# Seven-product block steps for a third of the feed-forward products of a 256-token encoder block

## The chip, the cores and the metric

The kernel runs on one core of one Trainium2 chip. The metric is device time in microseconds (us) of one launch; the time of a kernel is the median of its runs. Beside it there is one profiled execution with its own length, the span.

## The reference

One layer on 256 tokens of width 2048, in float32. Two feed-forward half-steps stand around a mixer:

```python
def rmsnorm(x, g):
    y = x * lax.rsqrt(jnp.mean(x * x, axis=-1, keepdims=True) + EPS)
    return y * g

def swiglu(h, w1, w3, w2):
    return (jax.nn.silu(h @ w1) * (h @ w3)) @ w2

x = x + 0.5 * swiglu(rmsnorm(x, ffn1_norm_g), ffn1_w1, ffn1_w3, ffn1_w2)
h = rmsnorm(x, mix_norm_g)
# projections h @ w_in, differential attention y_a, latent attention y_b
merged = sigmoid(ga) * (y_a @ w_branch_a) + sigmoid(gb) * (y_b @ w_branch_b)
x = x + merged @ w_out
x = x + 0.5 * swiglu(rmsnorm(x, ffn2_norm_g), ffn2_w1, ffn2_w3, ffn2_w2)
```

`w1` and `w3` are 2048 x 5632, `w2` is 5632 x 2048. The change touches the two `swiglu` half-steps; the mixer between them computes what it did.

## The kernel before, in words

**Products.** TensorE (PE) multiplies in float32r, a shortened float32, so every large product runs as three passes. An operand v is split into hi (v cast to float32r) and lo = v - hi, and hi*hi, hi*lo and lo*hi accumulate in one PSUM bank. The activations are the stationary operand: 128 x 128 blocks, transposed, already split. The weights are the moving operand, 128 rows by 512 columns in a matmul.

**One tile of weights.** `gemm` (line 124) walks down the rows of a weight matrix, two blocks of 128 rows at a time. SyncE (SP) issues a DMA of 512 KB into a raw tile, of which there are four (L135). `split` casts it on ScalarE (ACT, L105) and subtracts on VectorE (DVE, L106) into the tiles `wh` and `wl`, of which there are three each. Then come 12 matmuls: two row blocks, two blocks of 128 tokens, three passes (L144, L145, L146). Behind each tile one pending step of other work is issued, in the order in which steps were put off (`later`).

**A half-step.** `ffn` (line 231) cuts the 5632 hidden columns into 11 chunks of 512. A chunk is a gemm with `w1` (8 tiles, names f_u), Silu on ACT (L242), a gemm with `w3` (8 tiles, names f_v), and the product of the two on DVE (L246). Its transposes and their split (names f_t, f_ga, f_gb, f_gc) are put off into the next gemms. When all 44 blocks of hidden activations G are there, four gemms with `w2` over 22 tiles each follow (names f_d), and L261 adds half of the result to x, which stays in SBUF throughout. So a half-step has 11 x 16 + 4 x 22 = 264 tiles.

**What sets the order.** Each engine has its own queue and runs it in order. The order within a queue is that of the code as the scheduler lays it out; where an instruction needs another engine's result it waits on a semaphore, and everything behind it on its engine waits with it. Two PSUM banks of a gemm are in use while two others are free for the next, so that a gemm can begin before the last one has been read.

Of the kernel before, what the change touches and what calls it, by code (L numbers as in the profile page):

```python
# [71 lines left out]
def tile_block(ctx: ExitStack, tc: tile.TileContext, a, out: bass.AP):  # L72
# [51 lines left out]
    def gemm(w, n, kbs, hi, lo, name, due=None):  # L124
        """[S, n] = act @ w: w holds the rows of the blocks kbs, one block of 128 after
        another; hi/lo(kb, t) give the stationary operands.  Behind each weight tile
        one pending step of other work is issued; before tile `due` all of them."""
        po = [psum("mm", 4, f"{name}_{t}") for t in range(NT)]
        wv = w.rearrange("(kb p) n -> p kb n", p=P)
        for k0 in range(0, len(kbs), KT):  # L130
            if due is not None and k0 // KT == due:
                flush()
            kt = min(KT, len(kbs) - k0)
            raw = wp.tile([P, KT, n], F32, tag="raw", bufs=4, name=f"{name}_w")
            nc.sync.dma_start(out=raw[:, :kt], in_=wv[:, k0:k0 + kt, :])  # L135
            wh = wp.tile([P, KT, n], F32R, tag="wh", name=f"{name}_h")
            wl = wp.tile([P, KT, n], F32R, tag="wl", name=f"{name}_l")
            split(wh[:, :kt], wl[:, :kt], raw[:, :kt])
            for j in range(kt):
                kb = kbs[k0 + j]  # L140
                first, last = k0 + j == 0, k0 + j == len(kbs) - 1
                for t in range(NT):
# [2 lines left out]
                    nc.tensor.matmul(out=o, lhsT=hi(kb, t), rhs=wl[:, j], start=False, stop=False)  # L145
                    nc.tensor.matmul(out=o, lhsT=lo(kb, t), rhs=wh[:, j], start=False, stop=last)  # L146
# [79 lines left out]
    def chunk_done(x, t, c, T, g, pool, name):
        chunk_put(x, t, c, T, g, pool, name)
        chunk_sum(x, t, c, pool, name)

    # ---------------------------------------------------------------- feed forward  # L230
    def ffn(x, T, rstd, w1, w3, w2, tags, pool, done, name, first=None):
        hi, lo = operand(T)
        nf = DFF // P
        G = [big_tile(tags[0], f"{name}_ga"), big_tile(tags[1], f"{name}_gb"),
             pool.tile([P, 2, nf - 2 * KD, S], F32R, name=f"{name}_gc")]
        for c in range(DFF // NW):
            cs = slice(c * NW, (c + 1) * NW)
            p1 = first if c == 0 and first else gemm(w1[:, cs], NW, allk, hi, lo, f"{name}_u{c}")
            sg = []
            for t in range(NT):  # L240
                s = pool.tile([P, NW], F32, tag="silu", bufs=3, name=f"{name}_s{c}{t}")
                nc.scalar.activation(out=s, in_=p1[t], func=AF.Silu, scale=rstd[:, t:t + 1])  # L242
                sg.append(s)
            p3 = gemm(w3[:, cs], NW, allk, hi, lo, f"{name}_v{c}")
            for t in range(NT):
                nc.vector.scalar_tensor_tensor(out=sg[t], in0=p3[t], scalar=rstd[:, t:t + 1], in1=sg[t],  # L246
                                               op0=ALU.mult, op1=ALU.mult)

            def put(c, t, s):
                tp = transposes(lambda i: s[:, i * P:(i + 1) * P], 4, f"{name}_t{c}{t}")  # L250
                g, kk, sl = G[4 * c // KD], 4 * c % KD, slice(t * P, (t + 1) * P)
                split(g[:, 0, kk:kk + 4, sl], g[:, 1, kk:kk + 4, sl], tp)

            later(wait, *(partial(put, c, t, sg[t]) for t in range(NT)))
        ghi = lambda kb, t: G[kb // KD][:, 0, kb % KD, t * P:(t + 1) * P]
        glo = lambda kb, t: G[kb // KD][:, 1, kb % KD, t * P:(t + 1) * P]
        for c in range(D // NW):
            cs = slice(c * NW, (c + 1) * NW)
            po = gemm(w2[:, cs], NW, list(range(nf)), ghi, glo, f"{name}_d{c}", due=8)
            for t in range(NT):  # L260
                nc.vector.scalar_tensor_tensor(out=x[:, t, cs], in0=po[t], scalar=0.5, in1=x[:, t, cs],  # L261
                                               op0=ALU.mult, op1=ALU.add)
                done(t, c)
# [4 lines left out]
    with tc.tile_pool(name="f1", bufs=1) as pool:
        x = pool.tile([P, NT, D], F32, name="x1")
        T = big_tile("A", "hT1")  # L270
        def fetch(c):
            for t in range(NT):
                cs = slice(c * NW, (c + 1) * NW)
                nc.sync.dma_start(out=x[:, t, cs], in_=xin[:, t, cs])

        def put(c):
            for t in range(NT):
                chunk_put(x, t, c, T, "ffn1_norm_g", pool, f"i{c}{t}")

        rstd, step = rms_of_x("n1")  # L280

        def sums():
            for c in range(D // NW):
                for t in range(NT):
                    chunk_sum(x, t, c, pool, f"i{c}{t}")
            step()

        def start():
            for c in range(1, D // NW):
                fetch(c)  # L290
            put(1)

        fetch(0)
        gain_columns(0)
        put(0)
        later(start, wait, partial(put, 2), wait, partial(put, 3), sums, partial(gain_columns, 1))
        Tm = []

        def done1(t, c):
            if not Tm:  # L300
                Tm.append(big_tile("A", "hTm"))
            cs = slice(c * NW, (c + 1) * NW)
            nc.sync.dma_start(out=xdram[:, t, cs], in_=x[:, t, cs])
            later(partial(chunk_done, x, t, c, Tm[0], "mix_norm_g", pool, f"m{c}{t}"))

        ffn(x, T, rstd, a["ffn1_w1"][0], a["ffn1_w3"][0], a["ffn1_w2"][0], ("C", "D"), pool, done1, "f1")
        rstd, step = rms_of_x("n2")
        later(step)
        w_in = a["w_in"][0]
        hi, lo = operand(Tm[0])  # L310
        c_job = lambda j: gemm(w_in[:, O_C + j * 448:O_C + (j + 1) * 448], 448, allk, hi, lo, f"c{j}", due=4)
        first = c_job(0)

# [364 lines left out]
```

## Time and profile before

| | |
|---|---|
| median of 3 runs | 2444.77 us (2444.17 to 2445.04) |
| the profiled execution (its span) | 2442.6 us |
| feed-forward tiles, both half-steps | 528 |
| DMA, mean over the span | 185 GB/s |

The span begins with the program and ends with the last output transfer. A busy share counts an engine as busy while an instruction runs on it. PE records overlap, since matmuls are pipelined, so the pace of PE is read from the distance between the starts of instructions that follow it and not from the length of one record. In a table of waits a row names the waiting engine and what it waited for; then come the total, the number of times and the longest wait. SPq and POOLq are the queues of transfers that SyncE and GpSimd issue.

### The profile page before, as it was taken

What the parts mean: (1) busy time and instruction counts of PE and PEld (TensorE: products, weight loads), DVE (VectorE), ACT (ScalarE), POOL (GpSimd) and SP (SyncE); (2) the same over time, 40 slices, a digit from 0 to 9 for tenths busy, and PEclk for the clock granted to TensorE, in tenths of its full rate; (3) what the DMA queues carried; (4) which work ended last, traced back from release to release, by engine and by line L of the source; (5) the groups of instructions that cost most, each with busy time, mean ns of one, the idle gap of its engine ahead of it and who ended that gap; (6) DMA issues with size and microseconds to landing.
All of it is one profiled execution on the core that took longest, in us unless ns stands there. A gap on an engine that the chain in (4) does not pass through costs nothing.

```text
span 2442.6 us, 29136 instructions
## 1 busy us (share of the span) xinstructions
PE 2429.4 (99%) x11070; PEld 2013.9 (82%) x11070; DVE 1324.6 (54%) x1865; ACT 1111.9 (46%) x1378; POOL 96.0 (4%) x144
## 2 busy tenths in 40 slices
PE   8999999999999999999999999999999999999999
PEld 7888888888889888888888888888888888888887
DVE  5445445445555666666665665655545545444444
ACT  5444444434444555545545554444444444443333
POOL 1000000000000100001111210000000000000000
PEclk9999999999999999999999999999999999999999
DMA  7666666666667655655554556666666666666664
GB/s 222 186 190 191 188 190 189 190 190 199 199 200 202 186 164 171 179 168 164 150 158 151 156 157 183 189 223 184 188 190 190 189 190 189 188 191 190 202 205 153
DMA packets 235867, 450.92 MB, mean 185 GB/s; under 512 B 14612, under 2 KB 27600, under 8 KB 235600
## 3 DMA queue, kind: packets, MB, share of 16 engines
q1 hardware_dynamic: 234432, 448.40, 61.4%
q8 instruction: 86, 1.41, 0.2%
q10 hardware_dynamic: 1008, 0.66, 0.1%
q14 instruction: 53, 0.43, 0.1%
q0 software_dynamic: 288, 0.03, 0.0%
HBM read 444.83 MB, written 4.19 MB: 184 GB/s over the span
## 4 chain that ended last, share of the span: by engine, by line
PE 41%; issue 9%; POOL 2%; DVE 1%; DMA 0%; ACT 0%; POOLq 0%; ACTq 0%; DVEq 0%
PE f_u L146 3%; PE f_u L144 3%; PE f_u L145 3%; PE f_v L144 3%; PE f_v L145 3%; PE f_v L146 3%; PE f_d L146 3%; PE f_d L144 3%; PE f_d L145 3%; PE wo L146 1%; PE wo L144 1%; PE wo L145 1%; PE bb L146 1%; PE bb L144 1%; PE bb L145 1%
## 5 line engine op out<-in xcount | busy, mean ns | idle before, releaser
L106 DVE TENSOR_TENSOR f_v_l<-f_v_w,f_v_h 128x1024 fp32r<-128x1024 f32 x176 | 215.5, 1225 | 261.3 <-ACT f_v_h L105 261.3
L106 DVE TENSOR_TENSOR f_d_l<-f_d_w,f_d_h 128x1024 fp32r<-128x1024 f32 x176 | 215.7, 1225 | 243.3 <-ACT f_d_h L105 243.3
L106 DVE TENSOR_TENSOR f_u_l<-f_u_w,f_u_h 128x1024 fp32r<-128x1024 f32 x176 | 215.6, 1225 | 220.8 <-ACT f_u_h L105 220.8
L105 ACT CAST f_d_h<-f_d_w 128x1024 fp32r<-128x1024 f32 x176 | 185.6, 1055 | 289.2 <-PE f_d L146 276.0
L105 ACT CAST f_u_h<-f_u_w 128x1024 fp32r<-128x1024 f32 x176 | 185.3, 1053 | 282.5 <-PE f_u L146 175.6
L105 ACT CAST f_v_h<-f_v_w 128x1024 fp32r<-128x1024 f32 x176 | 185.1, 1053 | 239.6 <-PE f_v L146 168.3
L144 PE MATMUL f_u<-f_u_h,hT 128*128 128x512 f32 x704 | 278.4, 396 | 0.0
L145 PE MATMUL f_u<-f_u_l,hT 128*128 128x512 f32 x704 | 274.7, 390 | 0.5 <-DVE f_u_l L106 0.5
L146 PE MATMUL f_u<-f_u_h,hT 128*128 128x512 f32 x704 | 274.9, 391 | 0.0
L144 PE MATMUL f_v<-f_v_h,hT 128*128 128x512 f32 x704 | 273.9, 389 | 0.0
L145 PE MATMUL f_v<-f_v_l,hT 128*128 128x512 f32 x704 | 273.9, 389 | 0.0
L146 PE MATMUL f_v<-f_v_h,hT 128*128 128x512 f32 x704 | 273.9, 389 | 0.0
L146 PEld LDWEIGHTS f_u<-f_u_h,hT 128*128 128x128 f32 x704 | 132.3, 188 | 28.0
L145 PEld LDWEIGHTS f_u<-f_u_l,hT 128*128 128x128 f32 x704 | 132.6, 188 | 27.2 <-DVE f_u_l L106 0.7
L146 PEld LDWEIGHTS f_v<-f_v_h,hT 128*128 128x128 f32 x704 | 132.2, 188 | 27.5
L144 PEld LDWEIGHTS f_v<-f_v_h,hT 128*128 128x128 f32 x704 | 132.2, 188 | 27.4
L145 PEld LDWEIGHTS f_v<-f_v_l,hT 128*128 128x128 f32 x704 | 132.2, 188 | 27.4
L144 PEld LDWEIGHTS f_u<-f_u_h,hT 128*128 128x128 f32 x704 | 132.3, 188 | 26.1
L144 PE MATMUL da<-da_h,hTm 128*128 128x512 f32 x256 | 103.9, 406 | 0.0
L144 PE MATMUL f_d<-f_d_h,f_ga 128*128 128x512 f32 x256 | 100.5, 393 | 0.0
L146 PE MATMUL da<-da_h,hTm 128*128 128x512 f32 x256 | 100.2, 391 | 0.0
L106 DVE TENSOR_TENSOR da_l<-da_w,da_h 128x1024 fp32r<-128x1024 f32 x64 | 78.2, 1223 | 40.5 <-ACT da_h L105 40.1
(313 smaller groups left out, 4765.2 us busy)
## 6 DMA issues: line engine op xcount, KB each, us to landing
f_u_w<-in_ffn_w SPq DMA_DIRECT2D x176, 512.0 KB, 3.8
f_v_w<-in_ffn_w SPq DMA_DIRECT2D x176, 512.0 KB, 3.7
f_d_w<-in_ffn_w SPq DMA_DIRECT2D x176, 512.0 KB, 4.3
da_w<-in_w_in SPq DMA_DIRECT2D x64, 512.0 KB, 3.8
dav_w<-in_w_in SPq DMA_DIRECT2D x32, 512.0 KB, 3.8
ga_w<-in_w_in SPq DMA_DIRECT2D x32, 512.0 KB, 3.7
ba_w<-in_w_branch_a SPq DMA_DIRECT2D x32, 512.0 KB, 4.1
gb_w<-in_w_in SPq DMA_DIRECT2D x32, 512.0 KB, 4.3
```

What stands on the lines that cost most here:

```text
L105: nc.scalar.copy(out=hi, in_=src)
L106: nc.vector.tensor_sub(out=lo, in0=src, in1=hi.bitcast(F32))
L144: nc.tensor.matmul(out=o, lhsT=hi(kb, t), rhs=wh[:, j], start=first, stop=False)
L145: nc.tensor.matmul(out=o, lhsT=hi(kb, t), rhs=wl[:, j], start=False, stop=False)
L146: nc.tensor.matmul(out=o, lhsT=lo(kb, t), rhs=wh[:, j], start=False, stop=last)
```

## The change

**Two by two blocks.** The feed-forward products go through a new function, `gemm2`. It computes two output column halves of 512 (left and right) for both token blocks in one go. In the up-projection left is `w1` and right is `w3`; in the down-projection they are neighbouring halves of 1024 columns of `w2`. It walks down the rows in pairs of blocks, so a pair is a 2 x 2 block product: two token blocks by two row blocks, and two row blocks by two column halves. A pair is of one of two kinds.

- Kind P has the 8 block products of the textbook, 24 matmuls.
- Kind S has 7 block products of sums of blocks (Strassen's method in Winograd's form), 21 matmuls. Its weight sums are formed on the way in and its activation sums beforehand. Seven PSUM banks q1 to q7 hold the sums of products, one bank each and no second set, and are combined when they are read. Kind P adds into the banks q2 to q5 and uses differences of activation blocks, so that both kinds share the same reading.

**Which pairs.** An up-projection of 512 hidden columns has 8 pairs in the order PSPPSPSP, so 3 of 8 are S. The down-projection no longer waits for all of d_ff: after up-chunks 2, 5, 8 and 10 the `w2` rows of the chunks done so far are multiplied (6, 6, 4 and 6 pairs, 2, 2, 1 and 2 of them S, since the kinds by chunk are PS, PP, SP), once for each 1024 output columns. A half-step is thus 11 + 8 = 19 calls with 132 pairs, 47 of them S; both half-steps have 38 calls, 264 pairs and 94 S.

**The weight sums of an S pair.** Seven blocks are loaded instead of four. SP loads two right blocks into `sm` (L315, 512 KB), the second right block once more (L316, 256 KB) and two left blocks (L319, 512 KB). Two DMAs that GpSimd (POOL) issues add a block each to the two in `sm` (L321, L322: `accum_op=ALU.add`, 256 KB each). DVE makes the other two sums (L325, L326). Then four blocks of `raw` and three of `sm` are split. There are three raw, `wh` and `wl` tiles of four blocks each (twice as large as before); an S pair takes one raw and two of `wh` and `wl`. There are two `sm` tiles.

**Partial sums.** x no longer stays in SBUF. The result of a down-projection chunk other than the last is added to x in DRAM (`x_mid`) by an accumulating DMA from POOL, 1 MB each, 6 in a half-step (L421). For the last chunk x is loaded back in pieces (L393) and added on DVE.

**Small edits.** The factor 0.5 moves into the copy of the transposed hidden activations (L272, on ACT). Some tiles outside the half-steps go from two to one; the mixer's gemms keep their tiles of two blocks, now as halves of larger ones. The transposed sums of the second half-step's input are made while `w_out` is multiplied.

The diff, cut to its core (of the unchanged helpers and of the mixer nothing is shown):

```diff
+    SEVEN = (("q1", 0, "s", 1), ("q6", 5, "s", 0), ("q7", 2, "w", 1), ("q5", 4, "w", 0),
+             ("q2", 1, "s", 2), ("q3", 6, "s", 3), ("q4", 3, "w", 2))
+    PLAIN = (("q5", 2, 0), ("q2", 0, 1), ("q3", 4, 0), ("q4", 2, 1))
+    def put_pairs(pairs, srcs, gain, name):
...
+            tp = transposes(lambda i: src[:, i * P:(i + 1) * P], 4, f"tp_{name}{t}")
...
+                nc.scalar.activation(out=o, in_=i_, func=AF.Copy, scale=0.5)
...
+                if kind == "S":
+                    nc.vector.tensor_sub(out=g[:, 4], in0=g[:, 2], in1=g[:, 3])
+                    nc.vector.tensor_sub(out=g[:, 5], in0=g[:, 4], in1=g[:, 0])
+                    nc.vector.tensor_add(out=g[:, 6], in0=g[:, 1], in1=g[:, 5])
+                    nc.vector.tensor_sub(out=g[:, 2], in0=g[:, 0], in1=g[:, 2])
+                    n = 7
+                else:
+                    nc.vector.tensor_sub(out=g[:, 4:6], in0=g[:, 0:2], in1=g[:, 2:4])
+                    n = 6
+                split(T[:, 0], T[:, 1], g[:, :n])
+    def gemm2(left, right, pairs, name, due=None, x=None):
...
+            if kind == "S":
+                sm = pools["w7"].tile([P, 3, NW], F32, tag="sum", bufs=2, name=f"{name}_s")
+                nc.sync.dma_start(out=sm[:, 0:2], in_=right(k))
+                nc.sync.dma_start(out=raw[:, 3], in_=right(k)[:, 1])
+            else:
+                nc.sync.dma_start(out=raw[:, 0::3], in_=right(k))
+            nc.sync.dma_start(out=raw[:, 1:3], in_=left(k))
+            if kind == "S":
+                nc.gpsimd.dma_start(out=sm[:, 0], in_=left(k)[:, 0], accum_op=ALU.add)
+                nc.gpsimd.dma_start(out=sm[:, 1], in_=right(k)[:, 0], accum_op=ALU.add)
...
+                nc.vector.tensor_add(out=raw[:, 0], in0=sm[:, 0], in1=raw[:, 3])
+                nc.vector.tensor_add(out=sm[:, 2], in0=raw[:, 0], in1=raw[:, 2])
...
+                split(sh, sl, raw)
+                wh, wl = h4("w")
+                split(wh[:, 0:3], wl[:, 0:3], sm)
...
+            if i == lastS:
+                nc.scalar.copy(out=e11, in_=q["q1"])
+                nc.vector.tensor_add(out=e12, in0=q["q6"], in1=e11)
+                nc.vector.tensor_add(out=e21, in0=q["q7"], in1=e12)
...
+        nc.vector.tensor_sub(out=e12, in0=q["q5"], in1=e12)
+            nc.vector.tensor_sub(out=e22, in0=q["q5"], in1=e21)
...
+        nc.vector.tensor_add(out=x11, in0=q["q2"], in1=x11)
+        nc.vector.tensor_add(out=x12, in0=q["q3"], in1=x12)
+        nc.vector.tensor_add(out=x21, in0=q["q4"], in1=x21)
+    TKINDS, GKINDS = "PSPPSPSP", ("PS", "PP", "SP")
+    DOWN = {2: (0, 1, 2), 5: (3, 4, 5), 8: (6, 7), 10: (8, 9, 10)}
...
+                    nc.gpsimd.dma_start(out=xdram[:, :, ns], in_=ev, accum_op=ALU.add)
```

**How the queues change.** First VectorE of the kernel before, from the w1 gemm of one chunk to that of the next, in the first half-step. f_u_l and f_v_l are the subtractions of the weight split, f_s the gated product of a chunk, f_gb the split of its transposes.

```order
L106 TENSOR_TENSOR f_ga<-f_t_1504,f_ga 128x4x128
L106 TENSOR_TENSOR f_u_l<-f_u_w,f_u_h 128x1024 x2
L106 TENSOR_TENSOR f_v_l<-f_v_w,f_v_h 128x1024 x8
L106 TENSOR_TENSOR f_u_l<-f_u_w,f_u_h 128x1024 x2
L246 SCALAR_TENSOR_TENSOR f_s_1601<-f_v_0_1605,rstd_n_90,f_s_1601 128x512
L246 SCALAR_TENSOR_TENSOR f_s_1603<-f_v_1_1606,rstd_n_90,f_s_1603 128x512
L106 TENSOR_TENSOR f_u_l<-f_u_w,f_u_h 128x1024 x3
```

The same engine of the changed kernel where the up-projection of chunk 3 (f1_u3) meets that of chunk 4 (f1_u4). Names with _w_ are raw tiles, _s_ the tiles of sums, lp the lo part of a P pair, ls that of an S pair's raw tile, q the banks, e the tile into which they are read.

```order
L325 TENSOR_TENSOR f1_u4_w_1926<-f1_u4_s_1927,f1_u4_w_1926 128x512
L121 TENSOR_TENSOR f1_u3_lp_1844<-f1_u3_w_1840,f1_u3_hp_1843 128x2048
L343 TENSOR_TENSOR f1_u3_e_1598<-f1_u3_q6_1596,f1_u3_e_1598 128x512
L326 TENSOR_TENSOR f1_u4_s_1927<-f1_u4_w_1926 128x512
L344 TENSOR_TENSOR f1_u3_e_1598<-f1_u3_q7_1597,f1_u3_e_1598 128x512
L121 TENSOR_TENSOR f1_u4_lp_1892<-f1_u4_w_1888,f1_u4_hp_1891 128x2048
L352 TENSOR_TENSOR f1_u3_e_1598<-f1_u3_q5_1595,f1_u3_e_1598 128x512
L354 TENSOR_TENSOR f1_u3_e_1598<-f1_u3_q5_1595,f1_u3_e_1598 128x512
L359 TENSOR_TENSOR f1_u3_e_1598<-f1_u3_q2_1592,f1_u3_e_1598 128x512
L360 TENSOR_TENSOR f1_u3_e_1598<-f1_u3_q3_1593,f1_u3_e_1598 128x512
L361 TENSOR_TENSOR f1_u3_e_1598<-f1_u3_q4_1594,f1_u3_e_1598 128x512
L121 TENSOR_TENSOR f1_u4_ls_1936<-f1_u4_w_1926,f1_u4_hs_1935 128x2048
```

Where there was a plain run of subtractions with two products in it, the queue now holds the first sum of chunk 4's first S pair (L325) ahead of the subtraction for the last P pair of chunk 3, and the seven readings of the banks of chunk 3 among the subtractions for chunk 4.

Next TensorE. In the kernel before, a stretch of a w1 gemm with four transposes in it; f_u_0 and f_u_1 are the banks of the two token blocks.

```order
L144 MATMUL f_u_1_506<-f_u_h,hT_89 128x512
L145 MATMUL f_u_1_506<-f_u_l,hT_89 128x512
L146 MATMUL f_u_1_506<-f_u_h,hT_89 128x512
L158 MATMUL f_t_568<-ident,f_s_355 128x128 x4
L144 MATMUL f_u_0_505<-f_u_h,hT_89 128x512
L145 MATMUL f_u_0_505<-f_u_l,hT_89 128x512
L146 MATMUL f_u_0_505<-f_u_h,hT_89 128x512
```

In the changed kernel the end of the first S pair of a chunk and the beginning of the P pair behind it. hs, ls and hw, lw are the parts of the two split tiles of an S pair, hp and lp those of a P pair.

```order
L305 MATMUL f_u_q_1882<-f_u_hs,hT1s 128x512
L305 MATMUL f_u_q_1882<-f_u_ls,hT1s 128x512
L305 MATMUL f_u_q_1882<-f_u_hs,hT1s 128x512
L305 MATMUL f_u_q_1883<-f_u_hw,hT1s 128x512
L305 MATMUL f_u_q_1883<-f_u_lw,hT1s 128x512
L305 MATMUL f_u_q_1883<-f_u_hw,hT1s 128x512
L173 MATMUL tp_f_1964<-ident,f_u_e 128x128 x4
L305 MATMUL f_u_q_1884<-f_u_hp,hT1p 128x512
L305 MATMUL f_u_q_1884<-f_u_lp,hT1p 128x512
L305 MATMUL f_u_q_1884<-f_u_hp,hT1p 128x512 x2
```

A split tile now feeds 24 matmuls (P), 12 (the raw tile of an S pair) or 9 (its sums), where each fed 12 before.

More of the change, by code (lines that the diff above doesn't have):

```diff
@@ L52 @@
 NW = 512
-KT = 2
+KT = 4
 MASKED = -1.0e30
@@ L129, in gemm @@
         wv = w.rearrange("(kb p) n -> p kb n", p=P)
-        for k0 in range(0, len(kbs), KT):
-            if due is not None and k0 // KT == due:
+        for k0 in range(0, len(kbs), 2):
+            if due is not None and k0 // 2 == due:
                 flush()
[L133 to L138, printed above, removed]
+            kt = min(2, len(kbs) - k0)
+            if k0 % KT == 0:
+                full = [wtile("raw", F32, f"{name}_w"), wtile("wh", F32R, f"{name}_h"), wtile("wl", F32R, f"{name}_l")]
+            raw, wh, wl = (f[:, k0 % KT:k0 % KT + kt, :n] for f in full)
+            nc.sync.dma_start(out=raw, in_=wv[:, k0:k0 + kt, :])
+            split(wh, wl, raw)
             for j in range(kt):
@@ L226, in chunk_done @@
[L226 to L236, printed above, removed]
-            cs = slice(c * NW, (c + 1) * NW)
-            p1 = first if c == 0 and first else gemm(w1[:, cs], NW, allk, hi, lo, f"{name}_u{c}")
-            sg = []
-            for t in range(NT):
[L241 to L263, printed above, removed]
@@ L265, in tile_block @@
-    xdram = nc.dram_tensor("x_mid", (P, NT, D), F32, kind="Internal").ap()
[L268 to L312, printed above, removed]
@@ new lines, in pair_views, with turn, sums @@
+    def pair_views(t, n, w):
+        return [t[:, i * 2 * w:(i + 1) * 2 * w, :].rearrange("p (h s) k -> p h s k", h=2) for i in range(n)]
+    def put_pairs(pairs, srcs, gain, name):
+        f = []
+        def turn(t):
+            if t == 0:
+                f.append(pools["pt"].tile([P, 2, 7, P], F32, tag="pf", bufs=1, name=f"pf_{name}"))
+            src = srcs(t)
+            tp = transposes(lambda i: src[:, i * P:(i + 1) * P], 4, f"tp_{name}{t}")
+            o, i_ = f[0][:, :, 2 * t:2 * t + 2], tp.rearrange("p (a b) k -> p a b k", a=2)
+            if gain is None:
+                nc.scalar.activation(out=o, in_=i_, func=AF.Copy, scale=0.5)
+            else:
+                nc.vector.tensor_tensor(out=o, in0=i_, in1=gain.rearrange("p (a b) -> p a b", a=2).unsqueeze(3)
+                                        .to_broadcast([P, 2, 2, P]), op=ALU.mult)
+        def sums():
+            for a, (kind, T, _) in enumerate(pairs):
+                g = f[0][:, a]
+                if kind == "S":
[8 more added lines that the diff above has]
+                split(T[:, 0], T[:, 1], g[:, :n])
+        return [partial(turn, t) for t in range(NT)] + [sums]
@@ new lines, in tile_block, with fetch @@
+    xdram = nc.dram_tensor("x_mid", (P, NT, D), F32, kind="Internal").ap()
+    f1 = ExitStack()
+    enter(f1, "w7", bufs=1)
+    enter(f1, "ev", bufs=1)
+    enter(f1, "acc", bufs=1, space=bass.MemoryType.PSUM)
+    pool = pools["pt"] = f1.enter_context(tc.tile_pool(name="f1", bufs=1))
+    x = big.tile([P, NT, D], F32, tag="D", name="x1")
+    T = ffn_T("C", "A", "hT1")
+    def fetch(c):
+        for t in range(NT):
+            cs = slice(c * NW, (c + 1) * NW)
+            nc.sync.dma_start(out=x[:, t, cs], in_=xin[:, t, cs])
@@ new lines, in put, with sums @@
+    def put(c):
+        return ffn_put(x, T, c, "ffn1_norm_g", f"i{c}")
+    rstd, step = rms_of_x("n1")
+    def sums():
+        for c in range(D // NW):
+            for t in range(NT):
+                chunk_sum(x, t, c, f"i{c}{t}")
+        step()
+        nc.gpsimd.dma_start(out=xdram, in_=x)
+    fetch(0)
+    gain_columns(0)
+    for s in put(0):
+        s()
+    run = lambda *ss: (lambda: [s() for s in ss])
+    later(run(partial(fetch, 1), *put(1)), run(partial(fetch, 2), partial(fetch, 3)), run(*put(2)), run(*put(3)), sums,
+          partial(gain_columns, 1))
@@ new lines, in tile_block, with done1 @@
+    Tm = []
+    def done1(x, t, c):
+        if not Tm:
+            Tm.append(big_tile("A", "hTm"))
+        cs = slice(c * NW, (c + 1) * NW)
+        nc.gpsimd.dma_start(out=xdram[:, t, cs], in_=x[:, t, cs])
+        later(partial(chunk_done, x, t, c, Tm[0], "mix_norm_g", f"m{c}{t}"))
+    ffn(T, rstd, a["ffn1_w1"][0], a["ffn1_w3"][0], a["ffn1_w2"][0], "D", "C", pool, done1, "f1")
+    f1.close()
+    del pools["acc"], pools["w7"]
+    mixps = ExitStack()
+    enter(mixps, "ps", bufs=2, space=bass.MemoryType.PSUM)
@@ L315, in tile_block @@
+    ptx = ExitStack()
+    enter(ptx, "pt", bufs=1)
+    rstd, step = rms_of_x("n2")
+    later(step)
+    w_in = a["w_in"][0]
+    hi, lo = operand(Tm[0])
+    c_job = lambda j: gemm(w_in[:, O_C + j * 448:O_C + (j + 1) * 448], 448, allk, hi, lo, f"c{j}", due=4)
+    first = c_job(0)
+    ptx.close()
     ctx_merge = ExitStack()
@@ L360, in rotate @@
             h = ROPE // 2
-            u = pool.tile([P, 2, 2, ROPE], F32, tag="rot", bufs=2, name=f"u_{name}")
+            u = pool.tile([P, 2, 2, ROPE], F32, tag="rot", bufs=1, name=f"u_{name}")
             for i in range(2):
```

153 lines of the change are left out of this document (130 added, 23 removed).

## The prediction

> **What bounds the kernel now.** I read the busy shares first.
>
> ```profile
> span 2442.6 us, 29136 instructions
> PE 2429.4 (99%) x11070; PEld 2013.9 (82%) x11070; DVE 1324.6 (54%) x1865; ACT 1111.9 (46%) x1378; POOL 96.0 (4%) x144
> ```
>
> PE is busy for 99% of the span; VectorE (DVE) and ScalarE (ACT) have half of it free. Overlapping records can hide gaps, so the second view is busy time by stretches: PE, PEld, DVE, ACT, POOL, the granted clock, the DMA share, GB/s.
>
> ```profile
> 0.00:20.00 20.00, 12.89 (x56) 9.92 (x57) 11.83 (x17) 8.90 (x11) 4.96 (x14) 1.00 0.78 249
> 0.00:40.00 40.00, 32.89 (x144) 26.16 (x145) 22.41 (x28) 24.36 (x40) 8.24 (x22) 1.00 0.76 238
> 40.00:500.00 460.00, 460.00 (x2068) 380.66 (x2067) 228.99 (x207) 197.19 (x207) 0.00 (x0) 1.00 0.64 189
> ```
>
> The clock is full. All idle time of PE lies in the first 20 us: 40 - 32.89 = 7.1 us; the next 460 us have none. The waits say who is early.
>
> ```profile
> ACT f_d_h L105 <- PE f_d L146: 276.0, 167, 1.7
> DVE f_v_l L106 <- ACT f_v_h L105: 261.3, 173, 3.7
> SPq L135 <- DVE f_u_l L106: 418.8, 176, 4.2
> PE f_u L145 <- DVE f_u_l L106: 0.5, 1, 0.5
> ```
>
> Everybody waits for PE: ACT for a free split tile, DVE for ACT, the loads for a free raw tile; PE waits for weights once in 176 f_u tiles, for 0.5 us. So PE's instruction count sets the time. Its pace is the distance between subtractions in the down-projection, one per 12 matmuls:
>
> ```profile
> 519.58 1.23 DVE L106 TENSOR_TENSOR f_d_l<-f_d_w,f_d_h 128x1024 fp32r<-128x1024 f32 x1 [1.50 <-ACT f_d_h L105]
> 522.30 1.23 DVE L106 TENSOR_TENSOR f_d_l<-f_d_w,f_d_h 128x1024 fp32r<-128x1024 f32 x1 [1.50 <-ACT f_d_h L105]
> ```
>
> 2.72 us for 12, or 0.2267 us a matmul.
>
> **What goes.** Three gemms of 176 tiles with 12 matmuls are 6336 matmuls. The 94 S pairs leave out 3 each: 282 x 0.2267 = **-63.9 us**. Nothing overlaps with this term, since PE is the path. A P pair takes 24 x 0.2267 = 5.44 us, an S pair 4.76.
>
> **What DVE and ACT get.** The rows for their pieces (mean ns behind the comma):
>
> ```profile
> L106 DVE TENSOR_TENSOR f_u_l<-f_u_w,f_u_h 128x1024 fp32r<-128x1024 f32 x176 | 215.6, 1225 | 220.8 <-ACT f_u_h L105 220.8
> L106 DVE TENSOR_TENSOR f_v_l<-f_v_w,f_v_h 128x1024 fp32r<-128x1024 f32 x176 | 215.5, 1225 | 261.3 <-ACT f_v_h L105 261.3
> L106 DVE TENSOR_TENSOR f_d_l<-f_d_w,f_d_h 128x1024 fp32r<-128x1024 f32 x176 | 215.7, 1225 | 243.3 <-ACT f_d_h L105 243.3
> L106 DVE TENSOR_TENSOR mq_l<-mq_w,mq_h 128x768 fp32r<-128x768 f32 x24 | 23.0, 958 | 27.1 <-ACT mq_h L105 27.1
> L534 DVE TENSOR_TENSOR mg<-ba,mg 128x512 f32<-128x512 f32 x8 | 5.5, 690 | 2.8 <-PE ba L146 2.8
> L106 DVE TENSOR_TENSOR ybT<-mo,ybT 128x256 fp32r<-128x256 f32 x16 | 6.7, 418 | 0.2 <-ACT ybT L105 0.2
> L109 DVE SCALAR_TENSOR_TENSOR jda<-qk 128x128 bf16<-128x128 f32 x64 | 18.5, 289 | 5.2 <-ACT qk L411 3.6
> L246 DVE SCALAR_TENSOR_TENSOR f_s<-f_v,rstd_n,f_s 128x512 f32<-128x512 f32 x44 | 30.9, 744 | 0.0
> L105 ACT CAST f_u_h<-f_u_w 128x1024 fp32r<-128x1024 f32 x176 | 185.3, 1053 | 282.5 <-PE f_u L146 175.6
> L105 ACT CAST mq_h<-mq_w 128x768 fp32r<-128x768 f32 x24 | 20.0, 835 | 25.1 <-issue 16.2 <-ACT me L585 3.6 <-PE dav L146 3.5
> L242 ACT ACTIVATE f_s<-f_u,rstd_n 128x512 f32<-128x512 f32 x44 | 29.9, 690 | 19.7 <-PE f_u L146 19.7
> ```
>
> From 768 to 1024 elements DVE needs 267 ns more, 1.043 ns an element: a subtraction of 2048 is 2.29 us, of 1536 1.76, an addition of 512 0.69. ACT's cast grows by 0.85 ns an element: 1.93 and 1.49 us. An S pair costs DVE 2 x 0.69 + 2.29 + 1.76 = 5.43 us, longer than its own 4.76 us on PE; a P pair 2.29. One up-projection call of 5 P and 3 S: 27.7 us of these, 7 bank readings (4.8), 2 products (1.5), and the hidden activations' sums (one of 256 elements at 0.42, four of 128 at 0.29) and two splits (about 1.05 each), 3.7: 37.7 us. PE takes 183 x 0.2267 + 8 transposes of about 0.11 = 42.4 us. DVE goes from half to 89%, ACT stays near 60%. On average both still hide. Not at each place: the lo part of a P pair behind an S pair comes after 5.43 us of DVE work while PE has 4.76, so it uses up what was ahead; and the banks have no second set, so a new call's first use of q5 waits for L354. Walking through one call by these durations I get 0.2 us of stall (a choice of order, so an estimate).
>
> **Loads.** The rows (median us to landing; then the queue's packets, MB and share of 16 engines):
>
> ```profile
> f_u_w<-in_ffn_w SPq DMA_DIRECT2D x176, 512.0 KB, 3.8
> f_d_w<-in_ffn_w SPq DMA_DIRECT2D x176, 512.0 KB, 4.3
> x<-in_x SPq DMA_DIRECT2D x8, 256.0 KB, 7.1
> x_mid<-x SPq DMA_DIRECT2D x8, 256.0 KB, 5.1
> grow<-in_mix_norm_g POOLq DMA_DIRECT2D x1, 8.0 KB, 2.8
> grow<-in_mla_k_norm_g POOLq DMA_DIRECT2D x1, 0.5 KB, 7.1
> q1 hardware_dynamic: 234432, 448.40, 61.4%
> 1.29 0.72 POOL L187 DMA_DIRECT2D grow<-in_mix_norm_g  x1 [0.46 <-issue]
> ```
>
> A packet is 2 KB and takes 0.614 x 16 x 2442.6 / 234432 = 0.102 us of one engine. A P pair is 512 packets, an S pair 896, so a call's 5248 packets take 33.6 of its 42.4 us on 16 engines, 79% (before, 64% in the second stretch). That fits, with later landings. [...]
>
> Two places are tight. L325 stands in DVE's queue ahead of the last P pair's subtraction, and waits for L316, whose raw tile comes free only three pairs earlier: by my walk it has about 3.1 us, and 256 KB should land in about 3 (an estimate below the 3.8 of 512 KB; under crowding 5.1 and 7.1 are seen). Each us too late stalls DVE, and soon PE, at up to two places in an up-projection call. The accumulating pair has a chain of its own: load of `sm` (3.8 to 4.3), two issues on GpSimd (up to 0.72 each), landing (unknown: 2.8 to 7.1 by the nearest rows, small ones): 8 to 13 us, against about 13 from when L315 can go out. I take 5 us, by the row of the same size that also touches x in DRAM (5.1): 4 + 1.2 + 5 = 10.2, which hides.
>
> **The sum of stalls.** 0.2 us by the walk is the lower end for a call; half a microsecond late at both L316 places gives 1.0 as the upper. I take 0.6: 38 x 0.6 = **+22.8** (7.6 to 38). A gain is excluded, for PE's matmuls have no slack to lose.
>
> **Beginning, seams, end.** In the first call DVE must also make the sums and splits of x (eight of 0.69, four times 3.7: 20 us) beside 27.7 us of weights, 47.7 in all. I count it from 11 us, since x and weights are landing before (DVE was busy for 11.83 of the first 20 us; from 8 us it would be the lower end): 58.7 us, and most of one P pair on PE behind it, 62. PE's work there is 42.4 us and 32 more transposes, 46, so about 16 us are lost. Before, 7.1 were: 9 more, of which I take **+8** (5 to 10). At the seams (into the mixer, into the second half-step with new tiles for which the first S pair's chain has to run, twice the last chunk's loading of x back) I put 1.5 us each for four, **+6** (3 to 10), bounded by one landing each. The 12 additions into `x_mid` run beside 4 to 6 us of slack on GpSimd's queue, behind which the next `sm` sums stand: nothing, unless they land as late as in the second rival. At the end two readings stand behind the last bank as two products did before: nothing. The scaling by 0.5 and the mixer's smaller tiles: nothing, ACT has the time.
>
> Sum against the profiled span: 2442.6 - 63.9 + 22.8 + 8 + 6 = 2415.5. The median lies 2444.77 - 2442.6 = 2.2 above that span: **2418 us**. The likeliest case's own range is 2397 (all lower ends: -48.3) to 2439 (all upper ends: -5.9).
>
> **Rivals.**
>
> All hidden: order and slack absorb every stall, and only 8 us of beginning and seams stay: 2442.6 - 55.9 + 2.2 = 2389. For it: DVE and ACT have waited for PE everywhere so far. Against: three tight places with less than 1 us.
>
> The accumulating pair lands late: slower than before. Place: L325 at each S pair. Chain beyond 13 us means a landing over 7.5; every us more is paid 94 times. With 7.6 + 14 us of the other terms there are 42 us to lose, so it decides at 42 / 94 = 0.45 us, a landing of about 8 us. One us late gives 2442.6 - 63.9 + 21.6 + 94 + 2.2 = 2497. For it: 7.1 us is seen for 0.5 KB in GpSimd's queue. Against: that was the ninth of nine issues in a crowded start.
>
> DVE blocks GpSimd: an issue can't go on while a DVE subtraction of 2.29 us runs, so two issues cost up to 4.6 us more; a chain of 10.2 becomes 14.8, 1.8 late: 94 x 1.8 = 169, 2572 us. [...] The nine issues ran while DVE did next to nothing, so they don't decide it:
>
> ```profile
> 0.00:6.00 6.00, 1.30 (x5) 0.90 (x5) 0.18 (x1) 1.28 (x1) 4.96 (x14) 1.00 0.50 145
> ```
>
> DVE becomes the bound: it waits for the cast in each S pair (its sums come first, then 1.93 on ACT): 37.7 + 3 x 1.93 = 43.5 over 42.4, 1.0 more in each of 22 up-projection calls: 2418 + 22 = 2440. Against: P pairs' work can stand between.
>
> **Chances.** A difference under 0.2%, 4.9 us, is about what a measurement can't tell from none. Forecast 0.50 (0.02 of it within 0.2%); all hidden 0.12; DVE the bound 0.15 (0.07 faster, 0.06 same, 0.02 slower); late accumulation 0.17; GpSimd blocked 0.06. Faster 0.67, same 0.08, slower 0.25. The range of 2393 to 2497 leaves out most of "all hidden" (0.08), the worse third of late accumulation (0.05) and GpSimd blocked (0.06).
>
> **What would show it.** PE's waits in the new profile: forecast right if they are short ones at q5 behind L354, at lp behind an S pair and at L325 on L316. If PE idles under 5 us behind 70 us, all is hidden. If L325 waits for L321's or L322's landing 94 times, the late accumulation holds; if POOL's issues are far longer than 0.72 us, GpSimd is blocked. If DVE's busy share passes 95% between calls, it is the bound. The forecast is wrong if the pace of PE isn't 0.2267, or the sum of PE's idle time lies outside 25 to 65 us.

## The result and the profile after

The changed kernel takes 2542.35 us (median of 4 runs, 2539.24 to 2547.14) against 2444.62 before: a ratio of 1.0403, interval 1.0388 to 1.0418. It is 4% slower, where 1% faster was forecast, and lies outside the range.

The busy shares on the page of the changed kernel:

```profile
span 2543.6 us, 29605 instructions
PE 2417.9 (95%) x10788; PEld 1979.6 (78%) x10788; DVE 1757.0 (69%) x2269; ACT 1241.2 (49%) x1290; POOL 291.9 (11%) x365
```

The 282 matmuls are gone (11070 to 10788), but PE is idle for 2543.6 - 2417.9 = 125.7 us, where 13.2 were and the prediction had allowed for 25 to 65. It is also busy for nearly as long as before with fewer instructions: less 63.9, 2429.4 would be 2365.5, and it is 52 more. Two losses then, idle time and slow time. The waits show the first:

```profile
PE f_u_q L305 <- DVE f_u_lp L121: 47.5, 25, 4.8
PE f_d_q L305 <- DVE f_d_lp L121: 26.6, 11, 4.5
...
DVE f_u_w L325 <- DMA f_u_w<-in_ffn_w: 104.7, 28, 7.3
DVE f_d_w L325 <- DMA f_d_w<-in_ffn_w: 76.9, 22, 7.0
DVE f_u_w L325 <- DMA f_u_s<-in_ffn_w: 22.8, 5, 5.8
```

PE waits for the lo part of a P pair, whose data has nothing to do with any S pair. VectorE, which makes it, stands at L325, 50 times and for 181.6 us, for a raw tile (f_u_w, f_d_w); for the additions into the sums (f_u_s) it waits only 5 times. One place shows the chain. These are rows of GpSimd, SyncE, VectorE and PE around 410 us, each engine from its own timeline (start, duration, engine; rows in between left out):

```profile
403.29 1.10 POOL L421 DMA_DIRECT2D x_mid<-f_d_e  x1 [6.23 <-DVE f_d_e L361]
...
405.22 0.34 SPq L316 DMA_DIRECT2D f_d_w<-in_ffn_w  x1
...
402.92 2.28 DVE L121 TENSOR_TENSOR f_d_ls<-f_d_w,f_d_hs 128x2048 fp32r<-128x2048 f32 x1
405.11 1.75 DVE L121 TENSOR_TENSOR f_d_lw<-f_d_s,f_d_hw 128x1536 fp32r<-128x1536 f32 x1
413.36 0.69 DVE L325 TENSOR_TENSOR f_d_w<-f_d_s,f_d_w 128x512 f32<-128x512 f32 x1 [6.50 <-DMA f_d_w<-in_ffn_w]
413.97 2.29 DVE L121 TENSOR_TENSOR f_d_lp<-f_d_w,f_d_hp 128x2048 fp32r<-128x2048 f32 x1
...
412.01 0.39 PE L305 MATMUL f_d_q<-f_d_hp,f_gp 128*128 128x512 f32 x1
416.31 0.79 PE L305 MATMUL f_d_q<-f_d_lp,f_gp 128*128 128x512 f32 x1 [3.92 <-DVE f_d_lp L121]
```

The reload L316 is issued at 405.22, when the subtraction f_d_ls has ended and its raw tile is free, and just behind a 1 MB addition into `x_mid`. It isn't there until about 413.2, 8 us later. VectorE has only f_d_lw left ahead of L325, and from 406.9 to 413.4 it does nothing, because L325 heads its queue. The lp behind it, 2.29 us long, ends at 416.3, and PE starts in that moment after 3.92 us of waiting. The windows of the same place give the granted clock (third number from the end) and the DMA share (second):

```profile
404.00:412.00 8.00, 8.00 (x37) 6.61 (x36) 2.86 (x2) 2.38 (x2) 0.39 (x1) 1.00 1.06 280
414.00:416.00 2.00, 0.00 (x0) 0.00 (x0) 2.00 (x2) 0.78 (x1) 0.00 (x0) 0.75 0.54 210
416.00:418.00 2.00, 1.69 (x4) 1.40 (x5) 2.00 (x3) 1.12 (x1) 0.27 (x1) 0.50 0.26 33
418.00:420.00 2.00, 2.00 (x6) 1.52 (x6) 2.00 (x2) 0.00 (x0) 1.54 (x2) 0.50 1.00 337
422.00:424.00 2.00, 2.00 (x11) 1.64 (x10) 0.00 (x0) 0.00 (x0) 0.00 (x0) 1.00 0.99 254
```

The DMA engines are full up to 412. During the pause the clock falls to 0.50 and stays there for some 5 us after PE has begun again: 6 matmuls run in the two microseconds from 418, and 11 in those from 422 at full clock. PE counts as busy in that time. That is the second loss; the first run below tells how much of the 52 us belongs to it. The transfers, by kind:

```profile
f_u_w<-in_ffn_w SPq DMA_DIRECT2D x286, 512.0 KB, 5.8
f_u_s<-in_ffn_w POOLq DMA_DIRECT2D x132, 256.0 KB, 6.8
f_u_w<-in_ffn_w SPq DMA_DIRECT2D x66, 256.0 KB, 4.9
x_mid<-f_d_e POOLq DMA_DIRECT2D x12, 1024.0 KB, 10.4
```

The reload takes 4.9 us in the median (third row), where 3 had been expected, and the ordinary loads 5.8 instead of 3.8.

### The profile page after: what moved, and what is told of

Its sections match the earlier page's. It is cut to its first block, busy times and chain, and to the rows that moved or that the text cites. A ratio compares the mean times of both kernels' runs of the same rounds, so it can differ in the third digit from the quotient of the medians.

```text
span 2543.6 us, 29605 instructions
## 1 busy us (share of the span) xinstructions
PE 2417.9 (95%) x10788; PEld 1979.6 (78%) x10788; DVE 1757.0 (69%) x2269; ACT 1241.2 (49%) x1290; POOL 291.9 (11%) x365
## 3 DMA queue, kind: packets, MB, share of 16 engines
q1 hardware_dynamic: 246816, 470.95, 55.7%
q0 software_dynamic: 33136, 72.39, 15.4%
## 4 chain that ended last, share of the span: by engine, by line
PE 37%; DVE 5%; DMA 5%; issue 3%; ACT 2%; POOL 2%; DVEq 0%; SPq 0%; POOLq 0%; ACTq 0%
PE f_u_q L305 12%; PE f_d_q L305 5%; DMA f_u_w<-in_ffn_w 2%; PE ms L563 1%; DMA f_u_s<-in_ffn_w 1%; PE wo L161 1%; PE wo L159 1%; PE wo L160 1%; PE bb L161 1%; PE bb L160 1%; PE bb L159 1%; DVE f_u_lp L121 1%; DMA f_d_w<-in_ffn_w 1%; PE gb L160 1%; PE gb L159 1%
## 5 line engine op out<-in xcount | busy, mean ns | idle before, releaser
L120 ACT CAST f_u_hp<-f_u_w 128x2048 fp32r<-128x2048 f32 x110 | 210.3, 1912 | 276.3 <-PE f_u_q L305 225.2
L305 PE MATMUL f_d_q<-f_d_hp,f_gp 128*128 128x512 f32 x960 | 314.0, 403 | 3.2 <-ACT f_gp L120 3.2
L121 DVE TENSOR_TENSOR f_u_lp<-f_u_w,f_u_hp 128x2048 fp32r<-128x2048 f32 x110 | 251.6, 2288 | 68.2 <-ACT f_u_hp L120 67.9
L305 PE MATMUL f_u_q<-f_u_hp,hT1p 128*128 128x512 f32 x880 | 284.0, 398 | 0.0
L305 PE MATMUL f_u_q<-f_u_hp,hT2p 128*128 128x512 f32 x880 | 281.9, 395 | 0.6 <-ACT f_u_hp L120 0.6
L305 PEld LDWEIGHTS f_d_q<-f_d_hp,f_gp 128*128 128x128 f32 x960 | 187.2, 195 | 45.3 <-ACT f_gp L120 4.2
L305 PE MATMUL f_d_q<-f_d_lp,f_gp 128*128 128x512 f32 x480 | 194.3, 405 | 26.7 <-DVE f_d_lp L121 26.6
L305 PE MATMUL f_u_q<-f_u_lp,hT2p 128*128 128x512 f32 x440 | 174.8, 397 | 25.4 <-DVE f_u_lp L121 25.4
L305 PEld LDWEIGHTS f_u_q<-f_u_hp,hT1p 128*128 128x128 f32 x880 | 169.1, 192 | 36.2 <-issue 0.8
L305 PE MATMUL f_u_q<-f_u_lp,hT1p 128*128 128x512 f32 x440 | 175.5, 400 | 22.1 <-DVE f_u_lp L121 22.1
L120 ACT CAST f_d_hp<-f_d_w 128x2048 fp32r<-128x2048 f32 x60 | 114.7, 1912 | 135.7 <-PE f_d_q L305 93.3
L120 ACT CAST f_u_hw<-f_u_s 128x1536 fp32r<-128x1536 f32 x66 | 97.8, 1481 | 123.8 <-PE f_u_q L305 99.7
L321 POOL DMA_DIRECT2D f_u_s<-in_ffn_w x66 | 57.3, 869 | 805.1 <-DMA f_u_s<-in_ffn_w 386.7
L325 DVE TENSOR_TENSOR f_u_w<-f_u_s,f_u_w 128x512 f32<-128x512 f32 x66 | 45.4, 688 | 127.8 <-DMA f_u_w<-in_ffn_w 104.7
L121 DVE TENSOR_TENSOR f_u_lw<-f_u_s,f_u_hw 128x1536 fp32r<-128x1536 f32 x66 | 115.5, 1750 | 0.4 <-ACT f_u_hw L120 0.4
```

What stands on the lines that cost most here:

```text
L120: nc.scalar.copy(out=hi, in_=src)
L121: nc.vector.tensor_sub(out=lo, in0=src, in1=hi.bitcast(F32))
L305: nc.tensor.matmul(out=q[o], lhsT=x, rhs=b, start=o not in started, stop=end)
L321: nc.gpsimd.dma_start(out=sm[:, 0], in_=left(k)[:, 0], accum_op=ALU.add)
L325: nc.vector.tensor_add(out=raw[:, 0], in0=sm[:, 0], in1=raw[:, 3])
```

## The experiments

Each is an edit of the changed kernel. Theory H says that the place of L325 in VectorE's queue is the cause; A, the traffic; D, VectorE's load or the structure. Of each diff only the lines that matter are shown.

**First run: only the order.** One edge puts L325 behind the lo part of the P pair ahead of it (`last_lp` holds that subtraction).

```diff
-                nc.vector.tensor_add(out=raw[:, 0], in0=sm[:, 0], in1=raw[:, 3])
+                with tc.issue_after(last_lp[-1].ins) if last_lp else ExitStack():
+                    nc.vector.tensor_add(out=raw[:, 0], in0=sm[:, 0], in1=raw[:, 3])
```

> One ordering edge is added: the first weight sum of an S pair (L325) is issued on VectorE behind the lo part of the P pair ahead of it; work and traffic are unchanged. Theory H (head of the line: L325 waits for its late reload L316 in front of a subtraction that TensorE needs; TensorE pauses, and after a pause of over 2 us its granted clock is 0.50 for some 5 us): the 25 + 11 waits of TensorE for a P pair's lo part (74 us) shrink to under 20 us, the clock loss (52 us) to under 15, time 2435 to 2470. Rival A (the seven-block loads and the additions by DMA are simply too much traffic): the reload lands as late, the S pair itself now waits, time over 2510. Rival D (VectorE or the structure with one set of banks is the limit): no change, about 2540.

Measured: 2427.01 us, ratio 0.9927. A repetition with more runs gave 2427.26, ratio 0.9926 (0.9911 to 0.9941). The page, the waits and the reloads of this kernel, where L325 has become L328:

```profile
span 2425.1 us, 29520 instructions
PE 2386.3 (98%) x10788; PEld 1962.5 (81%) x10788; DVE 1760.7 (73%) x2269; ACT 1240.4 (51%) x1290; POOL 292.5 (12%) x365
```

```profile
PE f_d_q L307 <- DVE f_d_lp L121: 7.0, 3, 3.5
...
PE f_u_q L307 <- DVE f_u_lp L121: 2.0, 3, 0.9
...
DVE f_u_w L328 <- DMA f_u_s<-in_ffn_w: 10.2, 2, 5.8
```

```profile
f_u_w<-in_ffn_w SPq DMA_DIRECT2D x66, 256.0 KB, 4.8
...
f_d_w<-in_ffn_w SPq DMA_DIRECT2D x28, 256.0 KB, 4.8
```

The reload lands as late as before (4.8 us), but nothing waits for it any more, and 74 us of PE's waits have become 9. Between the two profiled runs lie 118.5 us. PE's idle time gives 125.7 - 38.8 = 86.9 of them, and the same 10788 instructions being busy for less, 2417.9 - 2386.3, gives 31.6: the low clock behind the pauses (mean granted clock 0.981 in the changed kernel, 0.996 here). H's cause holds, and the time is better than its range. Its clock figures were those of the place at 410 us; over the whole trace of the changed kernel 12 of 15 pauses of 2.1 to 4.8 us for a lo part were followed by a clock of 0.50, for 3.4 us behind nine and for 6.8 behind three (last section). One of its figures is missed: of the 52 us of longer busy time 2386.3 - 2365.5 = 20.8 stay, where under 15 were expected. A and D fail.

**Second: without the additions into the sums.**

```diff
-                nc.gpsimd.dma_start(out=sm[:, 0], in_=left(k)[:, 0], accum_op=ALU.add)
-                nc.gpsimd.dma_start(out=sm[:, 1], in_=right(k)[:, 0], accum_op=ALU.add)
```

> The two accumulating weight DMAs of an S pair (L321, L322) are left out, so its sums lack a block each; the rest is unchanged. Theory H: less traffic ahead of the reload L316, which lands in about 4 us instead of 5 to 8, L325 waits some 60 us instead of 200, time 2440 to 2490. Rival A: the additions are the cost, time 2400 to 2430. Rival D: about 2540.

Measured: 2474.96 us. The reload's landing in this kernel, and VectorE's largest waits in front of the first sum (L325 is L322 here; part of these waits are booked as "issue"):

```profile
f_u_w<-in_ffn_w SPq DMA_DIRECT2D x66, 256.0 KB, 2.8
```

```profile
DVE f_d_w L322 <- issue: 31.7, 9, 6.8
DVE f_u_w L322 <- DMA f_u_w<-in_ffn_w: 30.5, 17, 6.3
```

With less traffic the reload lands in the 3 us that the prediction had supposed, and still the kernel is slower than before: VectorE stands at this line for 97 us in all, where H had said some 60. So the additions make the reload late (4.9 us with them, 2.8 without), and cost 67 us in this order, but they are not the whole cause.

**Third: all four sums on VectorE.** The two accumulating DMAs and the reload go; two additions come.

```diff
+                nc.vector.tensor_add(out=sm[:, 0], in0=raw[:, 0], in1=raw[:, 1])
+                nc.vector.tensor_add(out=sm[:, 1], in0=raw[:, 3], in1=raw[:, 0])
                 nc.vector.tensor_add(out=raw[:, 0], in0=sm[:, 0], in1=raw[:, 3])
```

> All four weight sums of an S pair are made on VectorE (two more of 0.69 us a pair) from four loaded blocks; no reload, no accumulating weight DMA. Theory H: the sums wait only for loads that the P pairs have too; VectorE has 41.8 us of work in 42.4, some stall stays: 2430 to 2480. Rival A: 2400 to 2430. Rival D (VectorE): slower than the changed kernel, 2550 or more.

Measured: 2473.39 us, within H's range; it doesn't say yet whether order or VectorE's work is left. The sixth run below does.

**Fourth: all pairs of kind P.** The kinds are set to P throughout, and the reading of the banks loses q1, q6 and q7.

```diff
-            G[g] = [(k, v, 4 * g + 2 * i) ...
+            G[g] = [("P", v[:, :, 0:6], 4 * g + 2 * i) ...
```

> All 264 pairs are of kind P (8 products, 24 matmuls); the walk in pairs, the single set of banks and the partial sums into x_mid stay. It prices the structure without the seven-product form. Theories H and A: TensorE has all 6336 matmuls again and hardly waits, about 2450 to 2465. Rival D: the structure itself stalls, 2480 or more.

Measured: 2480.64 us. H and A expected less; here D is right: the structure alone costs 36 us. PE is idle for 35.8 us, 22.6 more than before, and busy for 13.6 us more with the same 11070 instructions (2443.0 against 2429.4, mean granted clock 0.995). Most of the idle time more is in these waits:

```profile
PE f_d_q L304 <- ACT f_gp L120: 10.1, 2, 5.1
PE f_u_q L304 <- ACT f_u_hp L120: 5.5, 2, 4.2
...
PE c L159 <- DVE f_x L354: 3.3, 1, 3.3
```

They are the seams: twice the last chunk, whose transposed activations are not ready when the last down-projection wants them, the second half-step's beginning, and the way into the mixer. Within the calls PE does not wait. From this kernel to the first run's, 2480.6 to 2427.0, the 94 S pairs bring 53.6 us of their 63.9.

**Fifth: the order and no additions.** The edits of the first and second run together:

```diff
-                nc.gpsimd.dma_start(out=sm[:, 0], in_=left(k)[:, 0], accum_op=ALU.add)
-                nc.gpsimd.dma_start(out=sm[:, 1], in_=right(k)[:, 0], accum_op=ALU.add)
+                with tc.issue_after(last_lp[-1].ins) if last_lp else ExitStack():
+                    nc.vector.tensor_add(out=raw[:, 0], in0=sm[:, 0], in1=raw[:, 3])
```

> The ordering edge of the first run, and the two accumulating weight DMAs left out (the sums lack a block each). If the order alone was the cause (H), traffic matters little once the order is right: within 12 us of the first run's 2427, though 67 us lay between the two kernels without the edge. Rival A: 40 us or more are saved, below 2390.

Measured: 2413.59 us. The additions cost 13 us with the right order and 67 without. H's 12 us is missed by little, A's 40 by far. What the additions take of the DMA engines is in the queues' rows, first of the first run's kernel, then of this one (packets, MB, share of 16 engines):

```profile
q1 hardware_dynamic: 246816, 470.95, 58.2%
q0 software_dynamic: 33136, 72.39, 16.1%
```

```profile
q1 hardware_dynamic: 246816, 470.95, 59.4%
q0 software_dynamic: 6064, 23.10, 4.3%
```

The additions are 33136 - 6064 = 27072 packets, and took (0.161 x 2425.1 - 0.043 x 2412.2) x 16 / 27072 = 0.169 us each. A plain packet took 0.582 x 16 x 2425.1 / 246816 = 0.092.

**Sixth: the order and four sums on VectorE.** The third run's kernel with its first two sums behind the lo part ahead:

```diff
+                with tc.issue_after(last_lp[-1].ins) if last_lp else ExitStack():
+                    nc.vector.tensor_add(out=sm[:, 0], in0=raw[:, 0], in1=raw[:, 1])
+                    nc.vector.tensor_add(out=sm[:, 1], in0=raw[:, 3], in1=raw[:, 0])
```

> All four weight sums on VectorE, from four loaded blocks, with the first two issued behind the lo part of the P pair ahead. H: its waits for a load in front of a needed subtraction go, from 2473 to 2415 to 2440. If VectorE's extra 4 us a call are the limit (rival D), it stays over 2460.

Measured: 2457.15 us, between the two expectations: the order gives 16 us here, and the 30 us that are left to the first run's kernel point to VectorE. The window from 100 to 550 us of the first run's kernel, then of this one:

```profile
100.00:550.00 450.00, 450.00 (x2010) 370.38 (x2010) 364.94 (x319) 242.05 (x175) 57.50 (x65) 1.00 0.91 262
```

```profile
100.00:550.00 450.00, 443.20 (x1943) 356.15 (x1942) 391.59 (x366) 230.62 (x167) 4.47 (x4) 1.00 0.64 202
```

PE runs 1943 instructions instead of 2010 in the same time, and VectorE is busy for 391.6 of 450 us. In the S pairs ScalarE's casts f_u_hs wait longer for VectorE's sums (252.9 us, 133.6 in the first run's kernel), and the subtractions f_u_ls longer for the casts (83.5 us against 58.6). I read this as one chain of sums, cast and subtraction that no longer hides; no run takes it apart. Traffic is at the old 0.64.

**Seventh: the changed kernel without the additions into x_mid.** L421 is left out; no ordering edge.

```diff
-                    nc.gpsimd.dma_start(out=xdram[:, :, ns], in_=ev, accum_op=ALU.add)
```

> The changed kernel (without the ordering edge) with the 12 accumulating DMAs of 1 MB into x_mid left out, so the partial sums of the down-projection are lost. H: the dozen longest pauses (3.4 to 4.8 us, behind a reload that shares the engines with such an addition) and the low clock behind them go: 2470 to 2500. Rival A (the additions of weights alone): 2530 to 2545.

Measured: 2494.36 us, as H said. Twelve transfers of 1 MB cost 48 us here, 4 us each. PE's waits for a lo part fall from 74 to 37 us, the longest from 4.8 to 2.5. The longest waits at L325 are now 4.6 and 5.0 us, where they were 7.3 and 7.0:

```profile
DVE f_u_w L325 <- DMA f_u_w<-in_ffn_w: 91.1, 33, 4.6
...
DVE f_d_w L325 <- DMA f_d_w<-in_ffn_w: 61.9, 23, 5.0
```

**Eighth: four S pairs in eight, with the order.**

```diff
-    TKINDS, GKINDS = "PSPPSPSP", ("PS", "PP", "SP")
+    TKINDS, GKINDS = "SPSPSPSP", ("PS", "PP", "SP")
```

> The ordering edge, and 4 of 8 pairs of an up-projection call of kind S, in the order SPSPSPSP. 22 S pairs more are 66 matmuls, 15 us, less. H: VectorE has 40.8 us of work against 41.7 on TensorE and the loads take 36 us (43 with additions counted twice), so some of it comes back as waits: 2415 to 2445. If traffic is the limit (A): over 2450.

Measured: 2508.96 us; over A's line. The 43 us of the expectation count an addition's packet twice; by the fifth run it took 0.169 / 0.092 = 1.8 times as long as a plain one. Now the additions themselves are waited for, at the S pair that opens a call:

```profile
DVE f_u_w L328 <- DMA f_u_s<-in_ffn_w: 64.5, 16, 8.7
...
PE f_u_q L307 <- ACT f_u_hs L120: 38.6, 9, 10.8
```

Two things changed at once, one S more and an S at a call's first place, so the run doesn't tell which of them did it.

**Ninth: L325 and L326 on GpSimd, without the edge.**

```diff
-                nc.vector.tensor_add(out=raw[:, 0], in0=sm[:, 0], in1=raw[:, 3])
+                nc.gpsimd.tensor_tensor(out=raw[:, 0], in0=sm[:, 0], in1=raw[:, 3], op=ALU.add)
```

> The two sums of L325 and L326 move from VectorE to GpSimd; no ordering edge, same loads and additions. It takes the late reload out of VectorE's queue in another way. H: TensorE's waits for a P pair's lo part (74 us) fall under 20 us, whatever the landing of the reload; GpSimd's queue now stands still at L325 and issues the next additions later, which may cost some of it: 2425 to 2500. If not the place in VectorE's queue but the late data or VectorE's load was the cause: 2520 or more.

Measured: 2453.89 us. GpSimd's waits:

```profile
POOL f_u_w L325 <- DMA f_u_w<-in_ffn_w: 263.8, 38, 10.4
...
POOL f_d_w L325 <- DMA f_d_w<-in_ffn_w: 198.0, 23, 10.0
```

The reload is waited for more than ever, 462 us, but by an engine behind which no P pair stands, and 88 us are won. PE's waits for a lo part, 74 us in the changed kernel, are nearly gone:

```profile
PE f_d_q L305 <- DVE f_d_lp L121: 1.5, 4, 0.6
...
PE f_u_q L305 <- DVE f_u_lp L121: 1.1, 2, 0.8
```

This confirms H by another way than the edge.

**Tenth: one addition by DMA, three sums on VectorE, with the order.** The sum in `sm[:, 0]` is still made by L321 on a block that is loaded once more; six blocks are moved instead of seven.

```diff
+                nc.sync.dma_start(out=sm[:, 0], in_=right(k)[:, 0])
+            nc.sync.dma_start(out=raw[:, 0::3], in_=right(k))
...
-                nc.gpsimd.dma_start(out=sm[:, 1], in_=right(k)[:, 0], accum_op=ALU.add)
+                    nc.vector.tensor_add(out=sm[:, 1], in0=raw[:, 3], in1=raw[:, 0])
```

> With the ordering edge: one weight sum by an accumulating DMA, three on VectorE, six blocks loaded for an S pair and no reload. It lies between two adds (2427) and none (2457) in traffic and in VectorE's work: 39.8 us of 42.4 in an up-projection call. 2425 to 2450 if VectorE's chain of sums, cast and subtraction is what made the kernel with none slower; under 2420 if traffic was the dearer of the two.

Measured: 2445.93 us, ratio 1.0004 (0.9993 to 1.0014). Between 2427 (two additions) and 2457 (none): once the order is right, the work of VectorE is dearer here than the traffic that spares it.

**Eleventh: the S pairs one place later, with the order.**

```diff
-    TKINDS, GKINDS = "PSPPSPSP", ("PS", "PP", "SP")
+    TKINDS, GKINDS = "PPSPSPSP", ("PS", "PP", "SP")
```

> The ordering edge, and the up-projection's pairs in the order PPSPSPSP, so that the first S pair of a call comes one place later. The pauses at the first S pair of a half-step (2.0 and 5.4 us, and the low clock behind the second) should shrink: 2415 to 2427. If the closer S pairs leave VectorE too little room: 2430 or more.

Measured: 2429.75 us (ratio 0.9920 to 0.9953), between the two expectations and not told apart from the 2427.26 of the repeated first run, for which stood:

> The kernel of the first run again, with more rounds: 2427, a ratio to the kernel before of 0.993.

The pause at the second half-step's first S pair became 4.6 us instead of 5.4; the late order is no gain.

## Why the prediction was wrong

**Reading of before; 63.9 us for 282 matmuls.** Right: without the wrong order 53.6 of them arrive.

**Durations of VectorE and ScalarE.** Right to within 0.02 us: 2288 and 1750 ns for the subtractions, 1912 and 1481 for the casts, against 2.29, 1.76, 1.93 and 1.49 us.

**The load of the DMA engines.** 79% was worked out from packets, each taken at 0.102 us. The first run's kernel shows 0.91 from 100 to 550 us, and the kernel before 0.64 from 40 to 500. An adding packet was dearer than a plain one, 0.169 us against 0.092 by the fifth run; how much of the way from 79% to 0.91 that is, no run takes apart. The upper end of the term for the stalls, 38 us, is in any case far from the 129 that the calls lost.

**The step that failed: "by my walk it has about 3.1 us, and 256 KB should land in about 3", and from it "half a microsecond late at both L316 places gives 1.0 as the upper".** The place was named (L325 ahead of a P pair's subtraction, waiting for L316), but both sides of the comparison were wrong. The time available was mostly 1.6 us, not 3.1: the reload goes out when f_d_ls or f_u_ls has freed the raw tile, and one subtraction of 1.75 us stands between that and L325 (405.22 to 406.86 in the place above). By the start times in the trace 31 of the 50 waits, 140 of their 182 us, lie in such places. And the landing was 4.9 and 5.3 us in the median, up to 8.9; the 5.1 and 7.1 us for 256 KB stood beside the estimate. So there were 50 waits of 3.6 us in the mean. The second run agrees: with a landing of 2.8 us, as supposed, VectorE still stood there for 97 us. With the edge the lo part, 2.29 us, stands ahead of this line too, and the waits of the first run's kernel have none for the reload there. So the term for 38 calls was not 22.8 us: with the structure at 36 and the matmuls at -63.9, the calls lost 2543.6 - 2442.6 + 63.9 - 36 = 129, of which the order alone takes back 118.5.

**What a pause costs was missing.** A microsecond of waiting was priced at one microsecond. In the changed kernel 12 of the 15 pauses of 2.1 to 4.8 us for a lo part were followed by a granted clock of 0.50, and 31.6 us of the 118.5 are that. The trace of before had a sign of it. The 1.00 in its first 20 us, read as a full clock, hides that its record of the clock begins only at 13.4 us; four transposes of the beginning took 1.12 us, as long as eight a little later (1.03), from which I estimate half the clock there:

```profile
4.95 1.12 PE L158 MATMUL tp_i<-ident,x 128*128 128x128 f32 x4 [1.67 <-DMA x<-in_x]
...
15.36 1.03 PE L158 MATMUL tp_i<-ident,x 128*128 128x128 f32 x8
```

**Beginning and seams: +14.** Mis-sized: 36 in the kernel of P pairs alone, of which 22.6 are idle time and 13.6 longer busy time. The last chunk, 5 us twice, was looked for at the loading of x, and sat at the transposes of the last activations.

**Rivals.** "All hidden" falls with the 125.7 us of idle PE. "The accumulating pair lands late" had the right line and the wrong transfer: the additions were waited for 5 times, the reload 50 times. "DVE blocks GpSimd" is refuted: issues of L321 took 850 to 949 ns and of L322 859 to 1252, and none stood for a subtraction's 2.29 us. At 417.74, for one, an issue of 0.91 us ran inside a subtraction that lasted from 416.78 to 419.07. "DVE becomes the bound" is not what happened; it is how I read the kernels with three or four sums there (2446 and 2457 us).

Open: why the reload is as late as 8 us behind one 1 MB addition, and whether a fourth raw tile would hide it; that wasn't tried.

## What to carry to other kernels

Where a scheduler lays out the queues, look for an instruction that waits for the latest transfer and stands ahead of work that the bottleneck needs: here one edge that adds nothing and removes nothing turned 1.040 into 0.993. Size such a wait from both ends: when the transfer can go out at all (here its tile came free one instruction ahead of the wait), and the slowest landing that the trace has for this kind, under the traffic of the new kernel and not by the median of the old. And price a change that makes the bottleneck pause with what the clock does behind the pause (31.6 of 118.5 us here).
